# Skipped expert parts: zero matmuls and separate conditions replaced by standing PSUM banks and nested conditions

## The chip, the cores and the metric

The kernel runs on one core of a Trainium2 chip. Its engines are TensorE (PE, matrix products, results in PSUM), VectorE (DVE), ScalarE (ACT), GpSimd (POOL) and SyncE (SP, which here issues the weight transfers). Each has its own instruction stream, and semaphores tie the streams together. PSUM has eight banks here, each a tile of 128 partitions by 512 float32. The metric is the device time of one execution in microseconds (us), lower is better.

## What is computed

Two layers of a diffusion backbone. Layer 0 handles 512 tokens (256 of context and 256 latent ones) with linear and grouped-query attention; of layer 1 only the 256 latent tokens are kept, behind a state-space mixer and a Fourier mixer. The change touches neither mixer. Behind each of them stands the same mixture of experts: a router picks two of 16 experts for each token, and the token gets the weighted sum of their gated feed-forward results.

```python
def route(h, router_w, router_b):
    s = jax.nn.sigmoid((h @ router_w).astype(F32))
    ...
    w = jnp.take_along_axis(s, idx, axis=1)
    return idx, w / jnp.sum(w, -1, keepdims=True)

def moe_ffn(h, idx, w, w_gate, w_up, w_down):
    ...
    def expert_block(args):
        xb, ei = args
        return (jax.nn.silu(xb @ w_gate[ei]) * (xb @ w_up[ei])) @ w_down[ei]
    ...
    y = yb[dest] * w.reshape(-1)[order][:, None].astype(h.dtype)
    return jnp.zeros_like(h).at[tok].add(y)
```

The model is 1024 wide, an expert's hidden layer 768. An expert's weights (9.4 MB) are the same however many tokens it gets. Worked out from the inputs, the 16 lists of tokens are 33 to 109 long in layer 0 (ten of them up to 64, four of 65 to 96, two longer) and 5 to 68 long in layer 1 (seven up to 32, eight of 33 to 64, one longer).

## The kernel before

**Lists and parts.** Each expert e = 2p + m is member m of pair p. Its list has room for 128 slots, cut into parts t = 0 to 3 of 32 slots. A part that lies beyond the list's end is skipped at run time: `when(rv, least, yes, no)` builds a condition on the list's length `rv`, on every engine that has work in it (L1460 in the profile). On PE such a condition is a compare-and-branch, the matmuls of the part, a jump, and behind them the other side, `no`: a matmul `z_mm` of a tile of bfloat16 zeros that clears the part's PSUM bank, since ACT and DVE read the bank in either case.

**An expert** is computed in two steps. `hidden` makes the gate and up products, a part t at a time, into a bank `gu..t` (32 float32 matmuls of 384 columns). In layer 0 the parts 0 and 1 are always computed, in layer 1 part 0 alone. `swiglu(t)` then reads the bank: ACT computes the SiLU of the gate half into a tile `sg`, and DVE (L1599) multiplies it with the up half and the gate of the token into `h`. There are two buffers `sg` in layer 0, and one in layer 1. `transposed` turns `h` into `hT`, and `down` makes the down product into two banks, `dp..0` for parts 0 and 1, `dp..1` for parts 2 and 3, each with conditions of its own; ACT and DVE (L1655) move them to `y`. An expert's `down` stands behind the next expert's `hidden` (L340 is the helper through which every matmul goes).

**A pair** has `features` (the gathered tokens' features, banks `xt`; the second half, `S` = 1, is conditional on the longer list of the pair exceeding 64) and `combine` (banks `cm`): one-hot matrices `oh` bring the rows `y` back to token order, four banks at a time (qh = 0, then qh = 1), and DVE adds each to the tokens' sums (L1562). The pair's `combine` is called by `between`, in the middle of member 1 of the next pair, between its parts 0, 1 and its parts 2, 3.

**Banks.** `ps(name, tag)` takes a bank from a pool: tag `pj` has two banks, `a` two, `b` four. `gu` takes `pj`, but member 0's parts 2 and 3 take `b`; `cm` takes `b`; `xt` and the list products `sl` take `a`; `dp` takes `b` for member 0 and `a` for member 1. A new tile in a bank waits until the readers of the bank's last tile are through.

**Order.** A scheduler lays out each engine's stream from the program and the tiles' dependences, so a condition's body can stand ahead of matmuls that the source has before it. Weights come by SP (L333, `wload`) in tiles of 1.5 MB into slots that are free again when PE has read them (names `ring`, `more` and `big` in the rows).

Of the kernel before, what the change touches and what calls it, by code (L numbers as in the profile page):

```python
# [8 lines left out]
F32 = mybir.dt.float32  # L9
# [25 lines left out]
# weight slots in the areas while the experts run  # L35
# [3 lines left out]
# ---------------------------------------------------------------- host layout  # L39
# [13 lines left out]
# parameters and constants: '' for the whole run, 'A' and 'B' for the mixers of the two layers  # L53
# [79 lines left out]
def host_layout(a):  # L133
# [41 lines left out]
    # (layer, third, k, half, p, 1024): sixteen units per third, in loads of three and one  # L175
# [19 lines left out]
    # (l, e, k quarter, p, k, tile, gate or up, feature): each tile holds a quarter of the features  # L195
# [3 lines left out]
    # (l, e, half, p, b, output): the partitions hold the b-th 32 features of each quarter  # L199
# [56 lines left out]
# generators, each a step at a time  # L256
# [6 lines left out]
# pieces of one tile  # L263
# [11 lines left out]
class Core:  # L275
    def __init__(self, tc, I, O, dbg=None, stop=None):
# [4 lines left out]
        self.pin = False  # L281

# [19 lines left out]
    # the four 16 KB areas b, o, a, x hold whatever lives across the parts of a layer  # L302
# [74 lines left out]
    # between the layers: LayerNorm, and the modulated input of layer 1  # L377
# [29 lines left out]
    # out = x * exp(-ln(1 + exp(-x))); t is scratch  # L407
# [6 lines left out]
    # a third of layer l's adaLN rows for both streams, as per-partition scalars mods[l][:, m, kt, stream]  # L414
# [57 lines left out]
    # acc = alpha * x + m2 * (o @ w_o); LayerNorm; v = modulated x for the experts; acc = alpha * x  # L472
# [31 lines left out]
    # layer 1's acc = alpha * x + m2 * (o @ w_o), over the features A of o, there before the others, and then B;  # L504
    # of the first N outputs all of A first
# [942 lines left out]
    def experts(self, l, nb, pm, rows, xg, zero, pos, number, aux):  # L1448
# [4 lines left out]
        def z_mm(p, n):  # L1453
            self.mm(p[:, :n], zero, zero.unsqueeze(1).broadcast_to([128, n // 128, 128]))

        def when(rv, least, yes, no=None):
# [3 lines left out]
            with tc.If(rv > least) as cmp:  # L1460
                yes()
# [305 lines left out]
```

## Time and profile before

| what | us |
|---|---|
| median of three runs | 1539.64 (1537.3, 1539.64, 1543.07) |
| span of the profiled execution | 1528.9 |
| median less that span | 10.7 |
| PE busy in the span | 1298.6 |
| experts of layer 0, stretch 390 to 858: PE busy | 431.6 of 468 |
| experts of layer 1, stretch 1100 to 1490: PE busy | 311.4 of 390 |

The profiled execution is one execution of the program with the hardware profiler on; its span goes from its first to its last instruction. The two stretches are those in which the experts of a layer run.

### The profile page before, as it was taken

What the parts mean: (1) busy time and instruction counts of PE and PEld (TensorE: products, weight loads), DVE (VectorE), ACT (ScalarE), POOL (GpSimd) and SP (SyncE); (2) the same over time, 40 slices, a digit from 0 to 9 for tenths busy, and PEclk for the clock granted to TensorE, in tenths of its full rate; (3) what the DMA queues carried; (4) which work ended last, traced back from release to release, by engine and by line L of the source; (5) the groups of instructions that cost most, each with busy time, mean ns of one, the idle gap of its engine ahead of it and who ended that gap; (6) DMA issues with size and microseconds to landing.
All of it is one profiled execution on the core that took longest, in us unless ns stands there. A gap on an engine that the chain in (4) does not pass through costs nothing. (4 is left out here: it accounts for less than half of the span.)

```text
span 1528.9 us, 28267 instructions
## 1 busy us (share of the span) xinstructions
PE 1298.6 (85%) x11753; PEld 799.5 (52%) x11754; DVE 755.5 (49%) x1899; ACT 417.4 (27%) x831; POOL 66.1 (4%) x68
## 2 busy tenths in 40 slices
PE   3999987996889889999988779989696778987774
PEld 0787643684334454665445348858442455544433
DVE  2756447776426233233344487567541544344534
ACT  3533243452112111111111243444321211121213
POOL 0000002011000000000000030030100000000000
PEclk8999988998899999999999989999898999999876
DMA  9322666044678978779987222652788998999931
GB/s 388 121 93 83 247 249 262 0 172 173 271 304 339 398 300 332 321 293 383 387 359 293 111 85 83 223 204 100 313 321 342 378 373 354 387 375 416 410 129 30
DMA packets 43700, 397.60 MB, mean 260 GB/s; under 512 B 4976, under 2 KB 9200, under 8 KB 12272
## 3 DMA queue, kind: packets, MB, share of 16 engines
q1 hardware_dynamic: 41200, 388.40, 63.1%
q0 software_dynamic: 1728, 4.20, 0.8%
q8 instruction: 158, 2.59, 0.7%
q10 hardware_dynamic: 576, 2.10, 0.3%
q14 instruction: 38, 0.31, 0.1%
HBM read 393.63 MB, written 3.15 MB: 260 GB/s over the span
## 5 line engine op out<-in xcount | busy, mean ns | idle before, releaser
L1599 DVE SCALAR_TENSOR_TENSOR h0p<-gu0p,gt0p,sg0p 128x192 f32<-128x192 f32 x64 | 25.1, 414 | 156.3 <-ACT sg0p L316 155.8
L1599 DVE SCALAR_TENSOR_TENSOR h1p<-gu1p,gt1p,sg1p 128x192 f32<-128x192 f32 x64 | 26.5, 414 | 142.2 <-ACT sg1p L316 142.2
L340 PE MATMUL gu1p<-more,big 128*32 128x384 f32 x976 | 87.2, 497 | 8.9 <-issue 5.1
L340 PE MATMUL gu0p<-big,xe0p 128*32 128x384 f32 x992 | 92.5, 494 | 0.2 <-DVE h0p L1599 0.2
L316 ACT ACTIVATE sg0p<-gu0p 128x192 f32<-128x192 f32 x64 | 19.7, 332 | 215.0 <-PE gu0p L340 211.8
L316 ACT ACTIVATE y0p<-dp0p 64x512 fp32r<-64x512 f32 x64 | 37.9, 591 | 147.9 <-PE dp0p L340 105.0
L340 PE MATMUL gu0p<-ring,xe0p 128*32 128x384 f32 x768 | 75.1, 490 | 1.5 <-ACT sg0p L316 0.8
L340 PE MATMUL gu0p<-more,xe0p 128*32 128x384 f32 x800 | 73.7, 488 | 0.9 <-issue 0.9
L1655 DVE TENSOR_TENSOR y0p<-dp0p,y0p 64x512 fp32r<-64x512 f32 x64 | 44.0, 688 | 58.2 <-ACT y0p L316 57.6
L340 PE MATMUL ada<-ring,small 128*32 128x512 f32 x344 | 60.1, 641 | 14.4 <-DMA ring<-in_ada 14.4
L316 ACT ACTIVATE sg1p<-gu1p 128x192 f32<-128x192 f32 x64 | 21.2, 330 | 183.5 <-PE gu1p L340 159.9
L340 PE MATMUL dp0p<-big,hT0p 128*32 128x256 f32 x792 | 59.6, 390 | 8.7 <-issue 6.1
L340 PEld LDWEIGHTS gu1p<-more,big 128*32 128x32 f32 x976 | 39.5, 112 | 51.6 <-issue 37.8
L1655 DVE TENSOR_TENSOR y1p<-dp1p,y1p 64x512 fp32r<-64x512 f32 x64 | 44.0, 688 | 42.9 <-ACT y1p L316 40.2
L340 PEld LDWEIGHTS gu0p<-big,xe0p 128*32 128x32 f32 x992 | 47.9, 111 | 32.9 <-issue 20.3
L316 ACT ACTIVATE y1p<-dp1p 64x512 fp32r<-64x512 f32 x64 | 37.8, 591 | 93.0 <-PE dp1p L340 49.1
L1562 DVE SCALAR_TENSOR_TENSOR big<-cm0p,mods,big 128x256 f32<-128x256 f32 x128 | 51.6, 476 | 20.0 <-PEq L1460 10.0
L340 PE MATMUL gu1p<-big 128*32 128x384 f32 x528 | 54.5, 521 | 4.0 <-issue 4.0
L340 PE MATMUL cm0p<-oh0p,y0p 128*128 128x512 f32 x192 | 55.2, 417 | 2.7 <-DVE big L1562 1.2
L316 ACT ACTIVATE big<-big 128x512 f32<-128x512 f32 (+2 forms) x81 | 44.7, 575 | 46.7 <-DVE big L626 19.4
L340 PE MATMUL zo<-zo,zw 128*128 128x256 f32 x384 | 54.6, 292 | 0.0
L340 PEld LDWEIGHTS zo<-zo,zw 128*128 128x128 f32 x384 | 48.6, 191 | 6.6 <-issue 4.3
(537 smaller groups left out, 2483.8 us busy)
## 6 DMA issues: line engine op xcount, KB each, us to landing
more<-in_egu SPq DMA_DIRECT2D x54, 1536.0 KB, 11.1
big<-in_egu SPq DMA_DIRECT2D x48, 1536.0 KB, 13.9
ring<-in_ada SPq DMA_DIRECT2D x27, 1536.0 KB, 7.3
ring<-in_ed SPq DMA_DIRECT2D x27, 1536.0 KB, 9.4
ring<-in_egu SPq DMA_DIRECT2D x26, 1536.0 KB, 10.1
big<-in_ed SPq DMA_DIRECT2D x21, 1536.0 KB, 10.6
more<-in_ed SPq DMA_DIRECT2D x16, 1536.0 KB, 10.6
ring<-in_odw SPq DMA_DIRECT2D x5, 1536.0 KB, 7.5
```

Of the source, the lines that this page charges most:

```text
L316: a = self.nc.scalar.activation(out, x, func, **kw)
L340: i = self.nc.tensor.matmul(out, lhsT, rhs, start=start, stop=stop, skip_group_check=True)
L1562: nc.vector.scalar_tensor_tensor(self.acc[:, h, f], y, self.mods[l][:, 5, f, h:h + 1], self.acc[:, h, f], op0=OP.mult, op1=OP.add)
L1599: nc.vector.scalar_tensor_tensor(H[:, t], p[:, 192:384], gt[:, 2 * m + t % 2, i, t // 2:t // 2 + 1], sg, op0=OP.mult, op1=OP.mult)
L1655: nc.vector.tensor_tensor(yl[r], dp[r], yh[r].bitcast(F32), op=OP.subtract)
```

## The change

Eight banks are opened once for each layer's experts (`open_banks`), under names such as `bank1pj0` or `bank0b3` (layer, tag, number). All eight are cleared there by one zero matmul each, with zeros in a corner of the routing's scratch. From then on `ps` hands the banks of a tag out in turn, and nothing clears them again: a skipped part leaves what an earlier tile wrote, and the gates and one-hot rows of absent tokens, which are zero, take it out of the result. `when` has no other side any more. The conditions of one list are nested: part 2 stands inside the condition of part 1 (in layer 1), part 3 inside that of part 2, in `hidden` and in `down`. Parts 2 and 3 of member 1 take `b` banks too. `combine` is called when all four parts and all four `swiglu` of member 1 have been. The part of `features` with S = 1 for pair 0 is called ahead of part 0 in layer 1. In the diff the comments that the change drops are left out, and so is the passing of `label`.

```diff
+    def open_banks(self, l):
+        zero = self.zero
+        self.nc.vector.tensor_scalar(zero, self.C('ident'), 0.0, None, op0=OP.mult)
+        banks = {tag: [self.ps(f'bank{l}{tag}{i}', tag) for i in range(n)] for tag, n in (('pj', 2), ('a', 2), ('b', 4))}
+        for b in banks['pj'] + banks['b'] + banks['a']:
+            self.mm(b, zero, zero.unsqueeze(1).broadcast_to([128, 4, 128]))
+        self.banks = banks
...
     def ps(self, name, tag='a'):
+        if self.banks:
+            b = self.banks[tag]
+            b.append(b.pop(0))
+            return b[-1]
...
-            zero = self.pm.tile([128, 128], BF16, name=f'zero{l}')
-            nc.vector.tensor_scalar(zero, self.C('ident'), 0.0, None, op0=OP.mult)
+            self.zero = r2[:, 704:768].bitcast(BF16)
...
-            with tc.If(rv > least) as cmp:
+            with tc.If(rv > least, label=label):
                 yes()
-            if no:
-                with cmp.Else():
-                    no()
...
-                    when(rv, 64, t_mm, lambda: [z_mm(p[c], 512) for c in range(2)])
+                    when(rv, 64, t_mm)
...
-            def part(t, j=range(4)):
-                p = self.ps(f'gu{l}{nm}{t}', 'pj' if m or t < 2 else 'b')
-                when(rv if t > l_first else None, 32 * t, lambda: [gu_mm(t, jj, p) for jj in j], lambda: z_mm(p, 384))
-                return p
-            l_first = 0 if l else 1
+            def part(t):
+                for j in range(4):
+                    gu_mm(t, j, p[t])
+            p = [self.ps(f'gu{l}{nm}{t}', 'pj' if t < 2 else 'b') for t in range(4)]
+            H = pm.tile([128, 4, 192], F32, tag='h', name=f'h{l}{nm}')
+
+            def third():
+                part(2)
+                when(rv, 96, lambda: part(3))
+
+            def second():
+                part(1)
+                when(rv, 64, third)
             if l:
-                p = [part(0)]
+                part(0)
                 middle()
-                p.append(part(1))
+                swiglu(0, p[0])
+                when(rv, 32, second)
+                swiglu(1, p[1])
             else:
...
-            for t in range(2):
-                swiglu(t, p[t])
-            between()
-            for t in (2, 3):
-                swiglu(t, part(t))
+                for t in range(2):
+                    swiglu(t, p[t])
+                first()
+                when(rv, 64, third)
+            for t in (2, 3):
+                swiglu(t, p[t])
+            between()
...
-                if S == 0:
-                    if l:
-                        when(rv, 32, lambda: d_mm(1), lambda: z_mm(dp, 512))
-                    else:
-                        d_mm(1)
-                    d_mm(0)
-                else:
-                    when(rv, 96, lambda: d_mm(1), lambda: z_mm(dp, 512))
-                    when(rv, 64, lambda: d_mm(0))
...
+            d_mm(0)
+            if l:
+                when(rv, 32, second)
+                evict(0)
+            else:
+                d_mm(1)
+                evict(0)
+                when(rv, 64, third)
+            evict(1)
```

On PE in layer 1, this is how the stream stands before where member 1 of pair 4 is computed. Names ending in 411 and 412 are its parts 1 and 2, `cm1p30` is qh = 0 and `cm1p31` qh = 1 of pair 3's `combine`.

```order
L340 MATMUL gu1p411_14449<-zero1_11155 128x384
L1460 UNCONDITIONAL_BRANCH
L340 MATMUL gu1p410_14414<-more13_11070,big_63 32x384 x8
L340 MATMUL cm1p300_14507<-oh1p300_14491,y1p3000_13992 128x256
...
L1460 UNCONDITIONAL_BRANCH
L340 LDWEIGHTS zero1_11155
L340 MATMUL gu1p412_14557<-zero1_11155 128x384
L1460 UNCONDITIONAL_BRANCH
L340 MATMUL cm1p310_14532<-oh1p302_14499,y1p3010_13994 128x256
L340 MATMUL cm1p310_14532<-oh1p302_14499,y1p3011_13995 128x256
L1460 COMPARE_AND_BRANCH
```

The same place now:

```order
L1471 COMPARE_AND_BRANCH x3
L354 MATMUL bank1b3_11037<-more12_10799,big_63 32x384 x8
L354 MATMUL bank1b3_11037<-more13_10800,big_63 32x384 x24
L1471 UNCONDITIONAL_BRANCH x2
...
L354 MATMUL bank1pj0_11030<-more13_10800,big_63 32x384 x8
L354 MATMUL bank1b0_11034<-oh1p300_14154,y1p3000_13601 128x256
...
L354 MATMUL bank1b1_11035<-oh1p300_14154,y1p3000_13601 128x256
...
L354 MATMUL bank1b2_11036<-oh1p301_14158,y1p3000_13601 128x256
...
L354 MATMUL bank1b3_11037<-oh1p301_14158,y1p3000_13601 128x256
```

The three conditions stand together ahead of parts 3, 2 and 1 (banks b3, b2 and pj1), the zeros are gone, and all of `combine` follows on the last products of part 0; two of its four banks, b2 and b3, are those of parts 2 and 3.

On DVE at that place, before (h1p41 is member 1 of pair 4; big is the tokens' sums):

```order
L1562 SCALAR_TENSOR_TENSOR big_63<-cm1p300_14507,mods1_77,big_63 128x256
L1599 SCALAR_TENSOR_TENSOR h1p41_14484<-gu1p411_14449,gt1p4_13907,sg1p411_14488 128x192
L1562 SCALAR_TENSOR_TENSOR big_63<-cm1p301_14508,mods1_77,big_63 128x256
L1460 UNCONDITIONAL_BRANCH
L1562 SCALAR_TENSOR_TENSOR big_63<-cm1p302_14509,mods1_77,big_63 128x256
L1562 SCALAR_TENSOR_TENSOR big_63<-cm1p303_14510,mods1_77,big_63 128x256
L1599 SCALAR_TENSOR_TENSOR h1p41_14484<-gu1p412_14557,gt1p4_13907,sg1p412_14592 128x192
```

And now:

```order
L1607 SCALAR_TENSOR_TENSOR h1p41_14008<-bank1pj1_11031,gt1p4_13522,sg1p411_14145 128x192
L1607 SCALAR_TENSOR_TENSOR h1p41_14008<-bank1b2_11036,gt1p4_13522,sg1p412_14148 128x192
L1607 SCALAR_TENSOR_TENSOR h1p41_14008<-bank1b3_11037,gt1p4_13522,sg1p413_14151 128x192
L1471 UNCONDITIONAL_BRANCH
L1570 SCALAR_TENSOR_TENSOR big_63<-bank1b0_11034,mods1_77,big_63 128x256
L1570 SCALAR_TENSOR_TENSOR big_63<-bank1b1_11035,mods1_77,big_63 128x256
L1570 SCALAR_TENSOR_TENSOR big_63<-bank1b2_11036,mods1_77,big_63 128x256
L1570 SCALAR_TENSOR_TENSOR big_63<-bank1b3_11037,mods1_77,big_63 128x256
```

The four `swiglu` of the expert stand together ahead of the pair's sums, where they stood between them. SP's transfers and POOL's work stand in the order of before.

## Rows read from the trace of the kernel before

**Rows 1.** The page's head: busy time, the granted TensorE clock in 40 slices.

```profile
span 1528.9 us, 28267 instructions
PE 1298.6 (85%) x11753; PEld 799.5 (52%) x11754; DVE 755.5 (49%) x1899; ACT 417.4 (27%) x831; POOL 66.1 (4%) x68
...
PEclk8999988998899999999999989999898999999876
```

**Rows 2.** Busy time by stretch: experts of layer 0, experts of layer 1.

```profile
core 0: us, PE busy (x) PEld busy (x) DVE busy (x) ACT busy (x) POOL busy (x), PEclk, DMA share, GB/s
390.00:858.00 468.00, 431.57 (x4904) 237.24 (x4906) 178.88 (x427) 75.06 (x161) 9.99 (x10) 0.98 0.80 324
1100.00:1490.00 390.00, 311.36 (x3361) 173.98 (x3364) 163.07 (x579) 74.85 (x155) 0.00 (x0) 0.92 0.84 343
```

**Rows 3.** The same stretches, instructions on the zero tiles alone (PE, PEld, DVE).

```profile
390.00:858.00 468.00, 15.55 (x46) 3.94 (x46) 0.00 (x0) 0.98 0.80 324
1100.00:1490.00 390.00, 25.52 (x74) 6.35 (x74) 0.00 (x0) 0.92 0.84 343
```

**Rows 4.** SP queue's waits, whole span: us in total, times, longest us.

```profile
SPq L333 <- PE gu0p L340: 234.4, 37, 18.6
SPq L333 <- PE gu1p L340: 193.2, 24, 21.4
```

**Rows 5.** PE's waits by releaser, 1110 to 1510 (layer 1): total, times, longest.

```profile
PE gu1p L340 <- issue: 25.7, 10, 5.0
PE dp1p L340 <- issue: 18.1, 8, 4.7
PE dp1p L340 <- PEq L1460: 13.6, 8, 5.3
...
PE gu1p L340 <- DVE big L1562: 3.1, 3, 1.6
PE gu1p L340 <- DMA big<-in_ed: 2.2, 1, 2.2
PE gu1p L340 <- DVE h1p L1599: 2.0, 2, 1.1
```

**Rows 6.** PE's waits by releaser, 390 to 858 (layer 0): total, times, longest.

```profile
PE dp0p L340 <- issue: 12.4, 7, 2.9
PE gu0p L340 <- issue: 8.1, 4, 4.6
PE dp0p L340 <- DVE big L1562: 3.3, 3, 1.1
PE dp0p L340 <- PEq L1460: 2.8, 5, 2.0
```

**Rows 7.** Conditions on PE, whole span: ns min/median/max of one branch.

```profile
L1460 PEldq COMPARE_BRANCH  x259: 65/208/5687, 391.0 to 1504.7; - x130
```

**Rows 8.** The page's table of DMA queues: packets, MB, share.

```profile
q8 instruction: 158, 2.59, 0.7%
```

**Rows 9.** PE's timeline at a short list of layer 1: start, us, instruction, [idle before].

```profile
1407.77 0.67 PE L340 MATMUL gu1p<-zero 128*128 128x384 bf16 x2 [1.65 <-issue]
1408.37 1.16 PE L340 MATMUL gu1p<-big 128*32 128x384 f32 x9
...
1412.49 0.72 PE L340 MATMUL dp1p<-zero 128*128 128x512 bf16 x2
1418.48 1.08 PE L340 MATMUL dp1p<-big,hT1p 128*32 128x256 f32 x8 [5.27 <-PEq L1460]
```

**Rows 10.** Timeline around a combine of layer 1.

```profile
1429.02 1.21 PE L340 MATMUL cm1p<-oh1p,y1p 128*128 128x256 f32 x8
1429.16 0.33 ACT L316 ACTIVATE sg1p<-gu1p 128x192 f32<-128x192 f32 x1 [4.38 <-PE gu1p L340]
1429.52 0.42 DVE L1599 SCALAR_TENSOR_TENSOR h1p<-gu1p,gt1p,sg1p 128x192 f32<-128x192 f32 x1 [3.32 <-ACT sg1p L316]
...
1431.17 0.32 PE L340 MATMUL gu1p<-zero 128*128 128x384 bf16 x1 [0.93 <-DVE h1p L1599]
```

**Rows 11.** Timeline around a combine of layer 0.

```profile
598.21 1.20 PE L340 MATMUL cm0p<-oh0p,y0p 128*128 128x512 f32 x4
...
600.75 3.23 DVE L1562 SCALAR_TENSOR_TENSOR big<-cm0p,mods,big 128x256 f32<-128x256 f32 x8 [0.81 <-PEq L1460]
601.15 1.06 PE L345 MATMUL xt0p<-const,xg 128*128 128x128 f32 x8 [0.53 <-PEq L1460]
```

**Rows 12.** The additions of the pairs' sums in layer 1: ns min/median/max.

```profile
L1562 DVE SCALAR_TENSOR_TENSOR big<-cm1p,mods,big x64: 473/476/485, 1184.9 to 1506.9; 128x256 f32<-128x256 f32 x64
```

More of the change, by code (lines that the diff above doesn't have):

```diff
@@ L1411, in moe @@
                 self.store(l, j)
-            self.experts(l, nb, pm, self.rows, self.xg, zero, *lists)
+            self.experts(l, nb, pm, self.rows, self.xg, *lists)
         self.slots = [i for i in self.slots if i in self.ring1]
@@ L1446, in spare, with experts @@
         return self.big[:, 12288 + 1024 * i:13312 + 1024 * i]
-    def experts(self, l, nb, pm, rows, xg, zero, pos, number, aux):
+    def experts(self, l, nb, pm, rows, xg, pos, number, aux):
         nc, tc = self.nc, self.tc
@@ L1451, in experts, with when @@
         NP = NE // 2
-        def z_mm(p, n):
-            self.mm(p[:, :n], zero, zero.unsqueeze(1).broadcast_to([128, n // 128, 128]))
-        def when(rv, least, yes, no=None):
+        def when(rv, least, yes, label=None):
             if rv is None:
@@ L1584, in load_d, with hidden @@
             return [self.wload(self.I['ed'][l, e, j], RING).rearrange('p (k f) -> p k f', k=3) for j in range(2)]
-        def hidden(nm, m, xe, gt, i, W, rv, middle, between):
+        def hidden(nm, m, xe, gt, i, W, rv, middle, first, between):
             def gu_mm(t, j, p):
@@ new lines, in d_mm, with third @@
+            def d_mm(t):
+                mp = 2 * m + t % 2
+                for kt in range(6):
+                    c, b = divmod(kt, 3)
+                    for x in range(4):
+                        q = x ^ mp
+                        self.mm(dp[t // 2][32 * x:32 * x + 32, (q % 2) * 256:(q % 2) * 256 + 256], hT[:, t, 32 * kt:32 * kt + 32],
+                                Wd[c][:, b, q * 256:(q + 1) * 256], start=kt == 0, stop=kt == 5)
+            def third():
+                d_mm(2)
+                when(rv, 96, lambda: d_mm(3))
@@ L1657, in outputs @@
+            d_mm(0)
[3 more added lines that the diff above has]
+            else:
+                d_mm(1)
+                evict(0)
+                when(rv, 64, third)
+            evict(1)
         def outputs(nm):
@@ L1694, in experts, with first @@
             Wd = load_d(e - 1) if e else None
-            def between():
+            def first():
                 if e == 0:
@@ L1701, in between @@
                         gathers(1)
+            def between():
                 if m == 1 and pend:
                     combine(*pend)
+            if l:
+                first()
             def middle():
@@ L1707, in middle @@
                     last[2] = transposed(*last[2])
-            H = hidden(f'p{p}{m}', m, xe, gt, i, W, rv, middle, between)
+            H = hidden(f'p{p}{m}', m, xe, gt, i, W, rv, middle, first, between)
             if m == 1 and p + 1 < NP:
```

24 lines of the change are left out of this document (9 added, 15 removed).

## Prediction

> **What bounds the kernel now.** I start at the page's head [rows 1]: PE is busy for 1298.6 of 1528.9 us, more than any other engine. The change touches only the two stretches with the experts, so I read those apart [rows 2]: in layer 0 PE is busy for 431.6 of 468 us at a granted clock of 0.98, in layer 1 for 311.4 of 390 us at 0.92. Is PE the bound there, or do the weights limit it? SP's queue answers: it stands waiting for PE to free the slots that `gu` reads, 234.4 us over 37 transfers for member 0 and 193.2 us over 24 for member 1 [rows 4]. The other way round PE waits for weights once in layer 1, for 2.2 us [rows 5]. So the weights come early, and PE's own time, with its idle time, sets the end of both stretches.
>
> What is that idle time? In layer 1 the large rows are not waits for an engine but "issue" and "PEq L1460": 25.7, 18.1 and 13.6 us in 10, 8 and 8 stalls, 57.4 us in 26 [rows 5]. In layer 0 they are 12.4, 8.1 and 2.8 us, 23.3 us in 16 stalls [rows 6]. They belong to the conditions: a branch takes 208 ns in the median, but up to 5687 ns [rows 7], and one such stall of 5.27 us stands behind the zero matmuls of a short list [rows 9]. Instructions come from memory in packets of 2.59 MB / 158 = 16.4 KB [rows 8]. I read the long stalls as jumps over a skipped part whose far end has not been brought in yet. That reading decides much below, and these rows do not prove it.
>
> **Part 1, the zeros.** In layer 0, 46 zero matmuls take 15.55 us, in layer 1, 74 take 25.52 us, some 0.34 us each, 41.1 us in all [rows 3]. Their weight loads lie beside other PE work and are not added. If PE is the bound, all of this is on the path. But a zero often stands next to a stall: in [rows 9] two follow one of 1.65 us and two others stand ahead of one of 5.27 us. While a zero runs, the instructions behind it go on arriving; without it, the stall next to it should grow by as much. I give each stall one zero as cover: 16 x 0.338 = 5.4 us in layer 0 and 26 x 0.345 = 9.0 us in layer 1. What is left is -10.1 and -16.5, **-26.6 us**. The ends: -41.1 where no zero is cover, and about -10 where all of layer 1's are.
>
> **Part 2, the conditions.** Nesting spares a short list the second and third compare. At the median of 208 ns [rows 7] some 64 spared ones (20 in layer 0, 44 in layer 1, counted from the lists' lengths) would be worth 13 us. PE's sequencer runs ahead of the matmuls, and [rows 5] shows only the long stalls, so I take 0 and keep -13 as the end. A jump now passes over up to three parts at once. The code that is passed over is the same in sum, and nothing stands between to be executed. What it does to the stalls no row shows. Two sides: the largest row, 25.7 us, could go, since code in the middle of a long jump need not be brought in; or it could come twice, since the far end is further off. I take **0**, from -25.7 to +25.7. [...]
>
> **Part 3, the pair's sums behind all parts.** In layer 1 the `combine` used to run while parts 2 and 3 were still to be dealt with, and its DVE additions alternated with `swiglu`. Now two of its four banks are those of parts 2 and 3, and they are free only when ACT and DVE have been through all four `swiglu`. With one `sg` buffer each takes 0.33 us on ACT and then 0.42 us on DVE [rows 10]: 4 x 0.75 = 3.0 us from the last product of part 0 to the last bank. The additions are queued on DVE behind these; at 0.476 us each [rows 12] the fourth ends at 4.9 us, and the last two matmuls of qh = 1 (0.15 us each, 1.21 us for eight [rows 10]) at 5.2. The 16 matmuls alone need 2.4 us. So PE waits for some 2.8 us per combine, with the products of the lists, the features and `down` queued behind it. Before, such waits were 3.1 + 2.0 us in the whole layer [rows 5], 0.7 for each of the seven combines that stand behind a nest (the last pair's stands alone at the end). The net is +2.1 us each. While PE waits its instructions go on arriving, so where a stall follows, some of it is repaid; I take 1.5 x 7 = **+10.5 us**, from 0 to 7 x 2.8 = 20.
>
> In layer 0 there are two `sg` buffers, and DVE alone sets the chain, 0.33 + 4 x 0.42 = 2.0 us. Four matmuls of `combine` (1.20 us) can go ahead, and the transposes `xt` (1.06 us) where they are not skipped [rows 11]; the wait is 0 to 0.8 us. The eight additions take 3.23 us of records in [rows 11], 8 x 0.476 = 3.8 us back to back, so that the last bank of qh = 0 is free at 2.0 + 3.8 = 5.8 us, when PE, at 0.3 us a matmul, would want it at about 5. The `down` of member 0 that follows uses the same banks and waits for the additions of qh = 1, as it already does before (3.3 us in three waits [rows 6]). I take +0.7 x 7 = **+4.9 us**, from 0 to 7 x 2 = 14.
>
> **Part 4, opening the banks.** Eight zero matmuls of 512 columns per layer, near 0.36 us each by the 0.72 us for two in [rows 9]: 2.9 us a layer. They stand where the lists are made, and partly wait for other engines anyway; I take +1 each, **+2 us**, from 0 to 6. The DVE operation that makes the zero tile only moves. The features with S = 1 of pair 0 move ahead of part 0 in layer 1; it is the same work in another place, once. The weight transfers keep their order on SP, and since they wait for PE [rows 4], they start earlier by what PE gains: nothing is late there for a gain of this size.
>
> **The sum.** -26.6 + 0 + 10.5 + 4.9 + 2 = -9.2 us. The profiled span of 1528.9 would become 1519.7. The median of the runs is 10.7 us above that span, and I carry this over unchanged: 1530.4, so **1530 us**, -0.6%. A measurement of this kernel can tell about 0.5%, 7.7 us, from no change, so the forecast lies just outside.
>
> **Rivals.** *A, the zeros were all on the path.* For it: PE is the bound in both layers, and in layer 0 its idle time is small. Then -41.1 + 17.4 (parts 3 and 4) = -23.7, 1516 us; with some long stalls gone too, as far as 1505. Against it: the zeros next to stalls [rows 9].
>
> *B, no change: layer 1 moves at the pace at which its instructions arrive.* For it: 57.4 us of layer 1's stalls are of that kind, and its zeros mostly stand between two jumps. Then layer 1's zeros give nothing and its new waits cost nothing either, beyond a third of the 10.5; what is left is -10.1 + 3.5 + 4.9 + 2 = 0, so 1540 us.
>
> *C, slower: the long jumps.* In layer 1 seven lists are up to 32 long, and each has a nest in `hidden` and one in `down` that is jumped over whole, 14 jumps. If the far end of each now costs one more arrival, at the mean of the largest row (25.7 / 10 = 2.6 us [rows 5]), that is +36 us, and with the forecast's -9.2 it gives 1566. It decides from (9.2 + 7.7) / 2.6 = 6.5 such jumps on; at eight of 14 the time is 1551. For it: the stall of 5.27 us, which came with a jump over far less [rows 9]. Against it: the old code had the same bytes to get past, in more jumps.
>
> That the change does not do what it says I exclude: in the new order the zeros are gone and the compares stand together.
>
> **How the numbers follow.** Forecast (1524 to 1538): 0.40. A (1505 to 1523): 0.21. B (1538 to 1546): 0.21. C (1547 to 1566): 0.18. Faster by over 0.5%, below 1532: all of A and two thirds of the forecast, 0.48. Within 0.5%, 1532 to 1547: the rest of the forecast and B, 0.34. Slower: C, 0.18. For 8 in 10 the range leaves out the lower half of A and the upper half of C: 1510 to 1553.
>
> **What the profile of the changed kernel would show.** Part 1: no zero matmuls but 16, and PE busy in layer 1's stretch down by about 25 us; if the stretch itself shrinks by that too, A is right, and if it stays as long with more "issue", B. Part 2: fewer than 259 branches executed; C shows as more branches of over 3 us, and as longer rows "PEq" for `gu` and `down`. Part 3: new rows where PE's `combine` waits for L1607 and L1570 of DVE, near 2 to 3 us per pair in layer 1 and under 1 in layer 0. The prediction is wrong if the stalls change by more than 15 us either way, since all of its other terms are small beside that; or if a lower granted clock in the emptier stretches slows the matmuls that remain.

## The result, and the profile after the change

The changed kernel takes 1590.21 us (median of four, 1587.38 to 1590.95), the kernel before 1541.36 us on the same chip (median of four): a ratio of 1.031, 95% interval 1.028 to 1.034. The forecast was 1530 us, range 1510 to 1553. The change costs 49 us, and sign and size were both wrong.

The head of the page after the change, the counterpart of [rows 1], and its queue of instructions, that of [rows 8]:

```profile
span 1585.6 us, 27894 instructions
PE 1309.3 (83%) x11648; PEld 804.6 (51%) x11649; DVE 758.1 (48%) x1899; ACT 414.7 (26%) x831; POOL 66.0 (4%) x68
...
q8 instruction: 156, 2.56, 0.6%
```

PE has fewer instructions, two packets of them fewer, and is busy for longer. To see where, I cut both traces at the same two events of each layer: the first and the last transposition of `h`, which begin each expert's down product. The columns are those of [rows 2]. Before:

```profile
418.30:837.60 419.30, 386.72 (x4484) 217.66 (x4476) 157.96 (x353) 66.67 (x147) 9.00 (x9) 0.99 0.83 339
1116.10:1491.10 375.00, 297.71 (x3243) 166.03 (x3235) 153.12 (x524) 69.88 (x147) 0.00 (x0) 0.92 0.85 350
```

After:

```profile
421.80:838.50 416.70, 375.90 (x4438) 206.99 (x4438) 158.28 (x353) 66.44 (x146) 8.90 (x9) 0.98 0.84 341
1120.40:1546.70 426.30, 314.16 (x3174) 180.07 (x3174) 153.87 (x521) 66.26 (x144) 0.00 (x0) 0.84 0.75 306
```

Layer 0 gains 2.6 us. All of the loss is in layer 1, 51.3 us. There PE's idle time goes from 77.3 to 112.1 us, and PE's busy time rises too, by 16.5 us, although the zeros (24.1 us of the 297.7) are gone: the remaining matmuls take 314.2 us in place of 273.6. The granted clock of the stretch falls from 0.92 to 0.84.

PE's conditions, as in [rows 7], are 193 in place of 259:

```profile
L1471 PEldq COMPARE_BRANCH  x193: 65/207/6075, 392.5 to 1561.5; - x193
```

PE's waits in layer 1, as in [rows 5]:

```profile
PE bank1pj L354 <- PEq L1471: 46.2, 21, 4.6
PE bank1b L354 <- DVE h1p L1607: 15.4, 14, 1.9
PE bank1a L354 <- DVE y1p L1673: 12.4, 5, 2.9
PE bank1a L354 <- issue: 11.5, 5, 2.9
PE bank1a L354 <- DVE tg1p L1518: 9.7, 6, 1.7
PE bank1b L354 <- DVE big L1570: 5.4, 8, 0.7
...
PE bank1pj L354 <- DVE y1p L1673: 4.5, 1, 4.5
PE bank1pj L354 <- issue: 4.5, 4, 3.5
```

The large rows "PEq" and "issue", which I take for stalls on instructions, are 46.2 + 11.5 + 4.5 = 62 us, where [rows 5] had 57.4; with the small rows, and between the same two transpositions, it is 62 us in both traces. What is new is DVE: 15.4 + 12.4 + 9.7 + 5.4 + 4.5 = 47 us, where [rows 5] had 3.1 + 2.0. Two of the waits stand at `combine` as forecast (h1p and big); two were not foreseen. With tg1p, the features of the next pair wait for DVE to read the list's product, which stands in the same bank; with y1p they wait for the eviction of `down`. The experiments show that these two do not come from the place of the sums: the wait for tg1p is there with the standing banks alone (21.2 us in before_banks), and that for y1p with the nested conditions (13.3 us in nest_mid, whose sums are in the middle; 1.0 us in flat, whose sums are behind, as in the kernel before). The timeline of PE at one `combine` shows the waits for h1p, big and tg1p in a row:

```profile
1192.08 0.74 PE L354 MATMUL bank1b<-oh1p,y1p 128*128 128x256 f32 x4
1194.74 0.50 PE L354 MATMUL bank1b<-oh1p,y1p 128*128 128x256 f32 x2 [1.93 <-DVE h1p L1607]
1195.56 0.53 PE L354 MATMUL bank1b<-oh1p,y1p 128*128 128x256 f32 x2 [0.31 <-DVE h1p L1607]
1196.83 2.07 PE L354 MATMUL bank1b<-oh1p,y1p 128*128 128x256 f32 x8 [0.74 <-DVE big L1570]
1199.05 1.84 PE L354 MATMUL bank1a<-aux,small 128*128 128x8 f32 x8
1202.50 3.77 PE L354 MATMUL bank1a<-small,xg 128*128 128x128 f32 x16 [1.60 <-DVE tg1p L1518]
```

The waits of this one pair come to 1.93 + 0.31 + 0.74 + 1.60 = 4.6 us. And the work between them is slow: the last line's 16 matmuls take 3.77 us, the same 16 before took 2.05:

```profile
1437.56 2.05 PE L340 MATMUL xt1p<-small,xg 128*128 128x128 f32 x16 [0.69 <-ACT big L316]
```

The granted clock is 0.52 over the slower sixteen (1202.50 to 1206.27) and 1.00 over the faster (1437.56 to 1439.61); the clock's records in these two traces say either 0.5 or 1. Ten microseconds at the first four pairs' sums after the change, from 3 to 4 us behind their first matmul on, columns as above:

```profile
1196.00:1206.00 10.00, 7.51 (x33) 7.04 (x32) 8.26 (x47) 0.00 (x0) 0.00 (x0) 0.50 0.76 322
1255.00:1265.00 10.00, 7.72 (x37) 7.36 (x38) 8.53 (x48) 0.32 (x1) 0.00 (x0) 0.54 0.62 262
1317.00:1327.00 10.00, 7.58 (x34) 6.83 (x33) 8.16 (x46) 0.00 (x0) 0.00 (x0) 0.59 0.76 324
1378.00:1388.00 10.00, 7.90 (x71) 7.00 (x75) 8.21 (x46) 1.21 (x3) 0.00 (x0) 1.00 0.82 348
```

Against them the first four pairs' sums of before:

```profile
1188.00:1198.00 10.00, 8.55 (x102) 5.80 (x105) 8.65 (x51) 3.19 (x6) 0.00 (x0) 1.00 0.98 410
1236.00:1246.00 10.00, 7.56 (x62) 6.70 (x60) 9.07 (x52) 2.28 (x4) 0.00 (x0) 1.00 1.00 421
1290.00:1300.00 10.00, 5.87 (x50) 4.21 (x53) 8.75 (x51) 3.00 (x6) 0.00 (x0) 1.00 0.97 411
1337.00:1347.00 10.00, 8.84 (x83) 7.59 (x85) 7.90 (x44) 2.92 (x6) 0.00 (x0) 1.00 0.84 330
```

The fourth pair after the change has the full clock too. At the other three of the seven pairs (ten microseconds from 1433, 1489 and 1536 after, from 1384, 1432 and 1480 before) the clock is 0.59, 0.52 and 0.66 after, 0.83, 1.00 and 0.56 before. So it is below 0.7 at six of seven pairs after and at one of seven before. This is not the mark of the sums' place alone: in before_banks below, with its sums in the middle, it is 0.66 at five of seven.

### The profile page after: what moved, and what is told of

Read it like the earlier page. It is cut to its first block, busy times and chain, and to the rows that moved or that the text cites. A ratio compares the mean times of both kernels' runs of the same rounds, so it can differ in the third digit from the quotient of the medians.

```text
span 1585.6 us, 27894 instructions
## 1 busy us (share of the span) xinstructions
PE 1309.3 (83%) x11648; PEld 804.6 (51%) x11649; DVE 758.1 (48%) x1899; ACT 414.7 (26%) x831; POOL 66.0 (4%) x68
## 5 line engine op out<-in xcount | busy, mean ns | idle before, releaser
L354 PE MATMUL bank1pj<-more,big 128*32 128x384 f32 x912 | 90.4, 531 | 25.8 <-PEq L1471 17.0
L1607 DVE SCALAR_TENSOR_TENSOR h0p<-bank0pj,gt0p,sg0p 128x192 f32<-128x192 f32 x32 | 13.3, 418 | 158.3 <-ACT sg0p L330 158.3
L354 PEld LDWEIGHTS bank1pj<-more,big 128*32 128x32 f32 x912 | 34.5, 118 | 72.9 <-issue 61.3
L354 PE MATMUL bank0pj<-big,xe0p 128*32 128x384 f32 x768 | 68.7, 486 | 2.1 <-PEq L1471 2.0
L354 PE MATMUL bank1pj<-big 128*32 128x384 f32 x528 | 53.7, 535 | 19.5 <-PEq L1471 19.2
L354 PE MATMUL bank0pj<-more,xe0p 128*32 128x384 f32 x672 | 62.2, 499 | 6.4 <-PEq L1471 5.3
L354 PE MATMUL bank1a<-small,xg 128*128 128x128 f32 x256 | 47.1, 361 | 22.1 <-DVE y1p L1673 12.4
L354 PE MATMUL bank0b<-oh0p,y0p 128*128 128x512 f32 x192 | 58.6, 428 | 7.0 <-DVE big L1570 4.2
L354 PE MATMUL bank0pj<-ring,xe0p 128*32 128x384 f32 x608 | 58.2, 488 | 4.3 <-PEq L1471 3.1
L1570 DVE SCALAR_TENSOR_TENSOR big<-bank0b,mods,big 128x256 f32<-128x256 f32 x128 | 51.6, 477 | 20.7 <-PEq L1471 11.5
L354 PEld LDWEIGHTS bank1a<-small,xg 128*128 128x128 f32 x256 | 43.9, 268 | 29.2 <-DVE y1p L1673 16.5
L354 PE MATMUL bank1b<-oh1p,y1p 128*128 128x256 f32 x144 | 32.9, 369 | 22.5 <-DVE h1p L1607 15.4
## 6 DMA issues: line engine op xcount, KB each, us to landing
big<-in_ed SPq DMA_DIRECT2D x21, 1536.0 KB, 10.1
```

The costliest lines, as they stand in the source:

```text
L354: i = self.nc.tensor.matmul(out, lhsT, rhs, start=start, stop=stop, skip_group_check=True)
L1570: nc.vector.scalar_tensor_tensor(self.acc[:, h, f], y, self.mods[l][:, 5, f, h:h + 1], self.acc[:, h, f], op0=OP.mult, op1=OP.add)
L1607: nc.vector.scalar_tensor_tensor(H[:, t], p[:, 192:384], gt[:, 2 * m + t % 2, i, t // 2:t // 2 + 1], sg, op0=OP.mult, op1=OP.mult)
```

## The experiments

Three suspects stood against each other: **W**, the place of the pair's sums; **J**, the jumps of the nested conditions; **Z**, the zeros, which may have been cover for stalls. The table has every timed kernel: its ratio to before, and from one profiled execution of each (so that no stretch has an interval) the layer 0 (L0) and layer 1 (L1) stretches cut as above, with PE in layer 1 (busy, of it zeros, idle, granted clock). The paragraphs behind it tell what each kernel is.

| kernel | ratio (95% interval) | L0 us | L1 us | busy (zeros) | idle | clock |
|---|---|---|---|---|---|---|
| before | 1 | 419.3 | 375.0 | 297.7 (24.1) | 77.3 | 0.92 |
| before_pad5 | 1.006 (1.004-1.009) | 425.7 | 385.0 | 306.2 (24.9) | 78.8 | 0.90 |
| before_pad11 | 1.009 (1.005-1.012) | 422.6 | 390.0 | 312.1 (24.2) | 77.9 | 0.88 |
| before_zz | 1.003 (1.001-1.005) | 417.7 | 387.2 | 314.3 (37.9) | 72.9 | 0.92 |
| before_banks | 1.006 (1.003-1.008) | 412.0 | 394.9 | 309.6 (24.5) | 85.3 | 0.88 |
| before_banks_xt | 1.001 (0.999-1.003) | 413.5 | 390.5 | 307.0 (24.4) | 83.5 | 0.88 |
| before_banks_l0 | 1.001 (0.998-1.004) | 417.6 | 389.4 | 308.1 (24.0) | 81.3 | 0.89 |
| flat_mid | 1.012 (1.006-1.017) | 420.3 | 396.0 | 300.5 (0) | 95.5 | 0.87 |
| flat_mid_xt | 1.007 (1.004-1.009) | 420.7 | 388.8 | 298.0 (0) | 90.8 | 0.90 |
| nest_mid | 1.014 (1.011-1.018) | 420.8 | 395.2 | 295.9 (0) | 99.3 | 0.87 |
| before_behind | 1.021 (1.018-1.024) | 428.1 | 397.4 | 319.9 (21.3) | 77.5 | 0.87 |
| before_behind_pj | 1.013 (1.010-1.017) | 432.7 | 397.7 | 319.9 (23.7) | 77.8 | 0.89 |
| before_behind_fill | 1.026 (1.021-1.031) | 431.7 | 404.3 | 322.8 (30.6) | 81.5 | 0.89 |
| before_behind_nest | 1.034 (1.029-1.040) | 423.7 | 416.6 | 332.3 (22.4) | 84.3 | 0.86 |
| flat | 1.024 (1.021-1.027) | 425.3 | 398.7 | 303.7 (0) | 95.0 | 0.85 |
| after_xt | 1.023 (1.018-1.028) | 419.8 | 411.3 | 307.5 (0) | 103.9 | 0.86 |
| after (the change) | 1.031 (1.028-1.034) | 416.7 | 426.3 | 314.2 (0) | 112.1 | 0.84 |
| after_pad5 | 1.026 (1.024-1.029) | 416.2 | 421.0 | 311.1 (0) | 109.9 | 0.86 |
| after_pad11 | 1.019 (1.016-1.022) | 416.8 | 418.0 | 314.8 (0) | 103.2 | 0.85 |

**The change taken apart.** flat_mid undoes the nesting and the place of the sums:

```diff
-                when(rv, 32, second)
+                when(rv, 32, lambda: part(1))
...
-                when(rv, 64, third)
+            between()
             for t in (2, 3):
+                p.append(self.ps(f'gu{l}{nm}{t}', 'pj' if m else 'b'))
+                when(rv, 32 * t, lambda: part(t))
                 swiglu(t, p[t])
-            between()
...
+            when(rv, 64, lambda: d_mm(2))
+            when(rv, 96, lambda: d_mm(3))
```

> The changed kernel with its conditions taken apart again (each part under a condition of its own) and the pair's sums back between parts 1 and 2 of member 1: of the change only the standing banks, and with them the missing zeros, are left. Theory W (the place of the pair's sums costs the time, by waits of PE for DVE): at or a little below before, ratio 0.985 to 1.00. Theory J (the nested conditions cost it, by jumps to code that has not arrived): the same, 0.985 to 1.00. Theory Z (the zeros were cover: without them PE idles more, and its clock falls): slower, 1.01 to 1.03.

The ratio is 1.012: the kernel is slower than before with little left but the standing banks and the missing zeros. At face value that excludes W and J as the whole of it.

nest_mid keeps parts 2 and 3 nested behind the sums:

```diff
-                when(rv, 64, third)
+            between()
+            p += [self.ps(f'gu{l}{nm}{t}', 'pj' if m else 'b') for t in (2, 3)]
+            when(rv, 64, third)
             for t in (2, 3):
                 swiglu(t, p[t])
-            between()
```

> The changed kernel with the pair's sums back between parts 1 and 2 of member 1; parts 2 and 3 stay nested in each other, as do all parts in the down product, but part 1 has a condition of its own in the gate and up products, since the sums stand behind it. No zeros. Theory W: 0.985 to 1.00. Theory J: most of the loss stays, 1.015 to 1.03. Theory Z: 1.01 to 1.03, the same as with the conditions apart.

The ratio is 1.014, the same as with the conditions apart. With the sums in the middle, nesting parts 2 and 3 and `down` costs nothing that can be told: the trace has fewer stalls on instructions (48 us against 70 in flat_mid) and, in their place, the wait for y1p, which flat_mid has not:

```profile
PE bank1a L354 <- DVE y1p L1670: 13.3, 5, 2.8
```

flat undoes the nesting alone, in `hidden` and in `down` (the diff is that of flat_mid, but `between()` stays behind and parts 2 and 3 stay in b banks).

> The changed kernel with its conditions taken apart again, the pair's sums still behind all four parts, and no zeros. Theory W: as slow as the change, 1.025 to 1.035. Theory J: the loss is gone, 0.99 to 1.005. Theory Z: 1.01 to 1.03.

The ratio is 1.024, just below what W expected and within what Z did: most of the loss is there without any nesting.

before_behind moves the sums in the kernel before, and gives parts 2 and 3 of member 1 b banks as in the change:

```diff
-                p = self.ps(f'gu{l}{nm}{t}', 'pj' if m or t < 2 else 'b')
+                p = self.ps(f'gu{l}{nm}{t}', 'pj' if t < 2 else 'b')
...
-            between()
+            first()
             for t in (2, 3):
                 swiglu(t, part(t))
+            between()
```

> The kernel before with one thing moved: the pair's sums stand behind all four parts of member 1 (whose parts 2 and 3 then use b banks, as in the change). Zeros, separate conditions and banks from the pools stay. Theory W: slower, 1.02 to 1.035. Theory J: 1.00 to 1.005. Theory Z: 1.00 to 1.01.

The ratio is 1.021, as W expected. The wait that I had priced is there, in layer 1's rows:

```profile
PE gu1p L340 <- issue: 32.1, 12, 4.0
PE cm1p L340 <- DVE h1p L1599: 14.8, 13, 2.0
```

but PE's idle time as a whole did not move (77.5 us against 77.3). What grew is the time of the matmuls, from 273.6 us without zeros to 298.6, at a clock of 0.87. (The shifted builds of before, told below, have 281 and 288 us, so not all of this growth need be the sums'.)

**The standing banks.** In flat_mid one wait stood out that no step had foreseen:

```profile
PE bank1a L354 <- DVE tg1p L1518: 21.8, 7, 3.6
```

The banks go out in a fixed turn, so the second half of the features gets the bank of the list's product, and waits for DVE to read it. Before, the pool gave it the bank of the first half, as its wait for `ACT big` in the row from 1437.56 suggests. before_banks puts the standing banks into the kernel before, zeros kept:

```diff
     def ps(self, name, tag='a'):
+        if self.banks:
+            b = self.banks[tag]
+            b.append(b.pop(0))
+            return b[-1]
...
+        self.open_banks(l)
...
```

> The kernel before with the standing banks of the change (opened once, handed out in turn) in place of the pools; zeros, separate conditions and the place of the pair's sums are those of before. Theory K (the fixed turn gives the second features bank the bank of the list's product, so that PE waits for DVE to read the list, 21.8 us in seven waits without zeros): 1.008 to 1.016, with that wait in the rows. Theory Z (the missing zeros are what cost 1.2%): 0.998 to 1.005.

The ratio is 1.006, between the two expectations, with the wait:

```profile
PE bank1a L352 <- DVE tg1p L1523: 21.2, 7, 3.6
```

flat_mid_xt and after_xt put both halves of layer 1's first features product into one bank:

```diff
+                if S == 0 and l:
+                    p.append(p[0])
+                    for c in range(2):
+                        t_mm(c, p[c])
+                        t_act(c, p[c])
+                    continue
```

> The kernel with standing banks, no zeros, separate conditions and the pair's sums in the middle, now with both halves of layer 1's first features product in one bank, the one that is not the list's. Theory K: the wait for the list's reads goes, and the time comes to 0.995 to 1.003. Theory Z: it goes too, but the time stays above before, 1.004 to 1.012.

> The changed kernel with both halves of layer 1's first features product in one bank, the one that is not the list's. Theory K: faster than the change by the 9.7 us of its wait and some clock, 1.018 to 1.026. Theory Z, and the theory that the place of the pair's sums sets it: 1.025 to 1.031.

The wait falls from 21.8 to 3.5 us in flat_mid_xt, and the ratio from 1.012 to 1.007, which is what theory Z expected; from the change it goes from 1.031 to 1.023, 12 us for a wait that falls from 9.7 to 1.6, as theory K expected. Both steps are no larger than what the place of the code alone moves (below), so they do not price the wait. before_banks_xt has the same with zeros and without the matmuls at the opening:

> The kernel before with the standing banks (no matmuls at their opening, since the zeros of skipped parts stay), and with both halves of layer 1's first features product in one bank, the one that is not the list's. With that wait gone (21.2 us in seven waits with the banks alone) and the zeros there, theory K expects 0.996 to 1.002; if standing banks cost something else too, 1.003 to 1.006.

The ratio is 1.001, but the wait did not go here (20.3 us in six): by the turn, the zeros of the second features product now mostly come to the list's bank. So the run did not test what it was built for. What it shows is that standing banks, wait included, come out at 1.001 and 1.006 in two builds: free within the scatter of builds.

**The zeros.** before_zz issues each zero matmul twice:

```diff
-            self.mm(p[:, :n], zero, zero.unsqueeze(1).broadcast_to([128, n // 128, 128]))
+            for _ in range(2):
+                self.mm(p[:, :n], zero, zero.unsqueeze(1).broadcast_to([128, n // 128, 128]))
```

> The kernel before with every zero matmul issued twice, some 120 more at 0.34 us, 41 us of PE work. Theory Z (zeros run while PE would stand still anyway): much of it is hidden, 1.00 to 1.012. If zeros are plain work on the path: 1.024 to 1.028.

The ratio is 1.003, 4.6 us. Zeros in its two stretches, cut at 390, 862, 1105 and 1510:

```profile
390.00:862.00 472.00, 24.10 (x92) 6.51 (x92) 0.00 (x0) 0.98 0.79 322
1105.00:1510.00 405.00, 40.41 (x148) 11.21 (x148) 0.00 (x0) 0.92 0.80 329
```

They keep PE busy for 64.5 us where [rows 3] had 41.1; of the 23.4 us added, 19 do not show in the time. Its code has moved too, so this holds within the scatter told below, and by stretches it is less clear: layer 1's grew by 12 us, no more than in the shifted builds without added zeros, and layer 0's shrank. The reverse says the same: flat_mid against before_banks (zeros away, a few calls in another order) has 24.5 us fewer of zeros in layer 1, and its stretch is 1 us longer, since PE idles 10 us more and the other matmuls take 15 us more. In layer 0 it is longer too (flat_mid, then before_banks; the first three numbers are the cuts and the length, the fourth PE's busy time):

```profile
421.80:842.10 420.30, 377.95 (x4438) 209.16 (x4438) 159.02 (x354) 66.81 (x147) 9.08 (x9) 0.98 0.83 338
423.30:835.30 412.00, 382.31 (x4473) 211.10 (x4473) 157.71 (x352) 66.64 (x146) 8.99 (x9) 0.99 0.84 344
```

In none of three pairs did leaving the zeros out make the kernel faster: 1.006 to 1.012 (before_banks to flat_mid), 1.001 to 1.007 (before_banks_xt to flat_mid_xt), and, with the standing banks put in as well, 1.021 to 1.024 (before_behind to flat).

**What makes the place of the sums dear.** before_behind_pj puts parts 2 and 3 of member 1 back into the pj banks (`'pj' if m or t < 2 else 'b'`), so that the sums find their banks free:

> The kernel before with the pair's sums behind all four parts, as in the run that gave 1.021, but with parts 2 and 3 of member 1 in the pj banks they had before. The sums then find all four b banks free. If it is the bank wait for swiglu (14.8 us in 13 waits of layer 1) that costs the time: 1.003 to 1.010, with a new wait of about 1 us per pair ahead of part 2's zeros. If it is that the sums' additions no longer alternate with other PE work (the queue on DVE, whatever the banks): 1.015 to 1.022.

The ratio is 1.013, between the two expectations: the bank wait of 14.8 us is replaced by one of 7.8 us ahead of `gu`, some of the loss goes and the rest stays. The step from 1.021 is again of the size that the place of the code moves. before_behind_fill puts work into the wait:

```diff
+                    if dd == 2 and qh == 0 and fill is not None:
+                        for _ in range(16):
+                            self.mm(fill[:, 384:512], zero, zero)
```

> The kernel before with the pair's sums behind all four parts (1.021), and in the middle of their first half, where PE waits for swiglu, 16 small zero matmuls into columns of a bank that nobody reads. They add PE work, some 1.5 us per pair, at the place of a wait of up to 2 us. If the granted clock falls because PE stands still there, and this is what makes the wait dear: faster than without them, 1.008 to 1.016, at a higher clock in layer 1. If the wait costs only itself: 1.020 to 1.025.

The ratio is 1.026. The wait of `cm1p` for h1p fell from 14.8 to 1.7 us, but the 16 matmuls have to wait for h1p themselves:

```profile
1202.72 1.05 PE L340 MATMUL gu1p<-zero 128*128 128x128 bf16 x16 [1.05 <-DVE h1p L1602]
```

They took 1.05 us in five of the seven pairs, behind a wait of 1 us each, 7.0 us in seven, so that of 14.8 us of standing still some 9 are left. The clock of layer 1 rose from 0.87 to 0.89 and the other matmuls went from 298.6 to 292.2 us, which the added zeros (9.3 us) and 4 us more of idle time used up. Since the wait was not closed, this does not settle whether standing still at that place is what lowers the clock.

before_behind_nest nests the conditions with the sums behind and the zeros kept:

```diff
-                when(rv if t > l_first else None, 32 * t, lambda: [gu_mm(t, jj, p) for jj in j], lambda: z_mm(p, 384))
...
+                when(rv, 32, second, zeros(1, 2, 3))
```

> The kernel before with the pair's sums behind all parts (1.021), its conditions nested as in the change, and its zeros kept: the other side of each condition clears the banks of all parts that it skips. If nesting costs time by itself (the changed kernel, 1.031, against the same with conditions apart, 1.024): 1.026 to 1.033. If it costs only because nothing runs at the far end of the longer jump, the zeros repair it: 1.015 to 1.023.

The ratio is 1.034, the slowest of all: this build lies 1.3% above before_behind, and zeros at the far end do not repair it. It is one pair of builds, and 1.3% is not far above what the place of the code moves.

**What a difference of a few us is worth.** before_again ran the kernel before once more:

> The kernel before once more, for a second profile: the span of the first, 1528.9 us, lies below all of its timed executions by more than the 2 us by which the spans of the other kernels lie below their times. If the first profile was of an uncommonly quick execution, the span is now 1535 to 1542 and layer 1's stretch between the first and the last transpose 380 to 388 us in place of 375.0; if not, 1527 to 1531 and 374 to 377.

Its span was 1536.4 us (time 1538.27), while layer 1's stretch was 376.5 us and layer 0's 422.3: the first profile was a quick execution as a whole, but not in layer 1. before_banks_l0 keeps the standing banks to layer 0:

> The kernel before with the standing banks in layer 0 alone, without matmuls at their opening; layer 1 keeps its pools. In two profiles with standing banks and zeros layer 0's stretch took 412.0 and 413.5 us against 419.3 in the first profile of before. If that is a gain of the banks: 0.993 to 0.998. If it is the scatter of executions: 0.998 to 1.002.

The ratio is 1.001, no gain. But its layer 1, whose streams are the same as before on all engines, took 389.4 us in the profiled execution. As far as the streams show, the one thing that differs there is where its code lies. So I shifted it, by tiny matmuls ahead of layer 1's routing (20 or 44 of them):

```diff
+            if l:
+                pad, one = self.ps('pad', 'pj'), self.C('ident')
+                for _ in range(44):
+                    self.mm(pad[:32, :2], one[:, :32], one[:, :2])
```

> The kernel before with 20 tiny matmuls (32 x 2) ahead of layer 1's routing, which shift all later code of PE against the 16.4 KB packets in which it arrives, by some 5 KB if a float32 matmul takes the 256 bytes that the packet count suggests; the experts' streams are untouched. With the banks in layer 0 alone, layer 1's streams were the same as before on every engine, and its stretch took 389.4 us against 375.0 and 376.5. Theory P (the place of the code against the packets sets a part of the stalls): layer 1's stretch 375 to 390 us, the time 1.001 to 1.010. If those 13 us have another cause: 375 to 378 and 1.000 to 1.003.

> The same with 44 tiny matmuls, a shift of some 11 KB. Theory P: a stretch that differs from that of the smaller shift by several us, within 373 to 392; without theory P 375 to 378, the time at most 1.004 by the matmuls themselves.

> The changed kernel with the same 20 tiny matmuls ahead of layer 1's routing. If the place of its code is unlucky and makes up much of its loss, the time falls to 1.015 to 1.025; if the loss stands for any place, 1.026 to 1.035, with layer 1's stretch within 10 us of 426.3.

> The changed kernel with the 44 tiny matmuls ahead of layer 1's routing: as for the smaller shift, 1.015 to 1.025 if its place was unlucky, 1.026 to 1.035 if not.

The layer 1 stretch of before, shifted by 20:

```profile
1127.60:1512.60 385.00, 306.21 (x3248) 179.30 (x3238) 153.16 (x524) 69.91 (x147) 0.00 (x0) 0.90 0.83 339
```

By 44:

```profile
1124.30:1514.30 390.00, 312.13 (x3243) 176.50 (x3235) 153.10 (x523) 69.81 (x146) 0.00 (x0) 0.88 0.82 336
```

That of the changed kernel, shifted by 20:

```profile
1123.40:1544.40 421.00, 311.11 (x3174) 178.43 (x3166) 153.93 (x521) 66.39 (x144) 0.00 (x0) 0.86 0.76 311
```

By 44:

```profile
1121.50:1539.50 418.00, 314.82 (x3174) 177.19 (x3174) 153.91 (x521) 66.27 (x144) 0.00 (x0) 0.85 0.77 313
```

The same experts' code runs layer 1 in 375 to 390 us before and in 418 to 426 us after, with nothing but its place changed; two executions of one build of before gave 375.0 and 376.5. The tiny matmuls themselves account for 1 to 3 us of the times, by the distance between the two layers' stretches. The 256 bytes that the expectation gives a matmul were an estimate: before, the packets of [rows 8] come to 220 bytes for each of the 11753 matmuls of [rows 1], and the shift in bytes was not measured. Of the two shifted builds of the changed kernel, one met each expectation. The ratios go over 1.000, 1.006, 1.009 and 1.031, 1.026, 1.019. The place of before is the luckiest of its three, that of the change the unluckiest of its three: the means are 1.005 and 1.025. Of the 3.1%, some 2% belong to the change, and some 1% to where its code happened to come to lie. In before the idle time hardly moves with the place (77.3 to 78.8 us); the time of the matmuls without zeros does (273.6, 281.3 and 287.9 us), with the clock (0.92, 0.90 and 0.88).

**What stands after that.** Single differences under about 1% are not told apart: whether the zeros' absence costs something (0.6% in two pairs), and what the nesting costs in the changed kernel (flat 1.024; the change 1.019 to 1.031). What stands as a group is the place of the sums: ten builds with the sums in the middle lie at 1.000 to 1.014 (mean 1.006), nine with the sums behind all parts at 1.013 to 1.034. The four of these nine that are not nested have a mean of 1.021, so that about 1.5%, 23 us, goes to the place of the sums; the five nested ones have 1.027. The pairs that differ in little else say the same: before_behind lies 1.2 to 2.1% above the three places of before, flat 1.2% above flat_mid.

## Why the prediction was wrong

**The bound.** That PE with its idle time sets the end held: the stretch grew as PE's idle time and matmuls did. What I left out is that PE's own pace is not fixed. I carried the matmuls' durations over and named a lower clock only in the last sentence. In layer 1 the remaining matmuls went from 273.6 to 314.2 us, 41 us (32 us between the means of the three places each), which is the largest single entry of layer 1's balance, and no term had it.

**Part 1, the zeros: the step that failed.** "I give each stall one zero as cover" left -26.6 us, the term that gave the forecast its sign. Measured, their removal gained nothing in three pairs of builds, and doubling them added 4.6 us for 23.4 us of work. The row on which I leaned, two zeros beside a stall of 5.27 us [rows 9], was the right one, but I let it count for one zero a stall. Without the zeros PE idles more, in layer 1 by 10 us (flat_mid against before_banks) and in layer 0, where I counted on -10.1 us, by 13 (42.4 us in flat_mid, 29.7 in before_banks). That a zero covers a stall beside it is a reading of these numbers. In the trace the branch of 5.51 us behind the stall of 5.27 us begins at 1412.65, while the two zeros of [rows 9] run (from 1412.49, 0.72 us); what they are worth there was not measured. Rival B had this mechanism, though in layer 1 alone.

**Part 2, the conditions.** I took 0 and bounded it by 25.7 us. With the sums in the middle it is 0 within the scatter (nest_mid against flat_mid). With the sums behind and zeros kept it is 1.3%, near 20 us, in one pair of runs at one place each. The stall rows do not carry it: 62 us before and after, counted alike. What nesting did bring is a wait that I had not looked for: with `down` nested, the features wait for its eviction (y1p, 12.4 us after the change, 13.3 in nest_mid; flat and flat_mid have only 1 us for y1p, at `combine`). Rival C's price, 14 arrivals of 2.6 us each, is not what happened, though branches did become long: by the trace, between the first and the last transposition of layer 1, PE had 7 branches of over 3 us before (34 us) and 13 after (64 us), in the shifted kernels 13 and 9 before, 13 and 6 after. The number hangs on the place of the code as much as on the nesting, and the idle time does not follow it. In both traces each of PE's branches of over 2 us (13 before, 22 after, the longest of 5.7 and 6.1 us) ends 1.3 to 1.5 us behind the end of a 16.4 KB packet of the instruction queue that began to move after the branch had begun. That these branches wait for the packet is a reading of these times, and it does not by itself give the sign of this change.

**Part 3, the sums behind all parts: right in kind, too small.** The mechanism was right and the size of its waits near: h1p and big cost 15.4 + 5.4 = 20.8 us in layer 1, where I took 10.5 and at most 20. For both layers I took 10.5 + 4.9 = 15.4 us; the groups of kernels that are not nested give some 23. I priced each wait at its own length and not at what follows it: at six of the seven pairs the clock around the sums is now 0.50 to 0.66, and in before_behind the matmuls grew while PE's idle time did not. That the waits lower the clock is argued and not shown. The wait for tg1p (9.7 us), missed as well, belongs to the standing banks: I followed the turn of the b banks and not that of the a banks.

In layer 0 the sum was near, but by luck. The stretch went from 422.5 us (the mean of 419.3, 422.3, 425.7 and 422.6, all with the same layer 0) to 416.6 (416.7, 416.2 and 416.8), -5.9 where I had -10.1 + 4.9 = -5.2. The terms are not these: by single profiles, leaving out the zeros went with +8.3 us (before_banks to flat_mid), moving the sums behind with +5.0 (flat_mid to flat), and nesting with -8.6 (flat to the change), for which I had 0, and the standing banks, for which I had none, with -10.5, -9.0 and -4.9 in three builds (before_banks, before_banks_xt, before_banks_l0, against the mean of before).

**Part 4, the opening.** No run showed it apart: the matmuls at the opening stand ahead of the stretches, and the distance from layer 0's last transposition to layer 1's first went from 278.5 (279.1 in the second profile) to 281.9 us.

**The sum.** "The median of the runs is 10.7 us above that span, and I carry this over unchanged": the other executions lie some 2 us above their spans (1587.38 for 1585.6, 1538.27 for 1536.4). The 10.7 was a quick execution, not an overhead. This did not turn the sign. From -9.2 to +49 us there are 58 to account for. By the numbers above some 27 are the zeros, 8 the place of the sums, and 15 to 17 the place of the code; the last 6 to 8, for the nesting and the standing banks, are not told apart. These are estimates, each uncertain by about 1%, 15 us, as single builds are.

**What is open.** Three things stay open: why the granted clock falls where the code lies differently, at the same idle time; whether the standing still at the sums or something else brings the clock down there; and the cost of nesting by itself. No version faster than both was found: before_banks_xt and before_banks_l0 are the same as before.

## What to carry to other kernels

Work that fills a bank or a wait between jumps can be nearly free, as the zeros were here (4.6 us of time for 23.4 us more of them): ask what stands beside it before counting its removal as a gain, and try doubling it, which is one run. When work is moved behind all of its neighbours, follow the turn of every bank it takes, and read the granted clock of the matmuls behind a wait (0.50 to 0.66 at six of seven pairs here) before pricing the wait at its own length. Before a difference of 1% in a kernel with many jumps is put down to an edit, shift its code, as the 20 and 44 tiny matmuls did here (by up to 0.9% and 1.2%), and time it again.

## What the runs showed of the hardware that was not expected

- The place of the code: 20 or 44 tiny matmuls ahead of layer 1's routing, which take 1 to 3 us themselves, moved the whole kernel before by +0.6% and +0.9%, and the changed one by -0.5% and -1.2%.
- The granted clock was 0.50 over a whole stretch of 10 us in which PE was busy for 7.5 us, behind waits of 0.3 to 1.9 us, and at 1.00 in one of before in which PE was busy for 5.9.
- Zero matmuls in bfloat16 between jumps: 23.4 us more of them came with 4.6 us more of time (1.003, in one build).
